# Keys, queries and values of three recurrent scans, turned by VectorE and DMA instead of TensorE

## The chip, the cores and the metric

The kernel runs on one core of a Trainium2 chip. The metric is the device time of one execution in microseconds; lower is better. TensorE (PE) multiplies matrices and writes into PSUM, eight banks of 128x512 floats. VectorE (DVE), ScalarE (ACT) and GpSimd (POOL) work on elements; SyncE (SP) issues every DMA of this kernel, in program order.

## The reference

One layer of a decoder with three kinds of recurrent heads, for a prompt of 1024 tokens with 16 learned tokens in front, and for 8 sequences of 8 tokens. Cut to what matters:

```python
h = _rmsnorm(x, norm_w)
proj = h @ w_in                              # (tokens, 8984): q, k, v, gates and z of 16 heads
conv = silu(causal_conv4(concat[bq, bk, bv]))
qb, kb, vb = _l2norm(q) * 128 ** -0.5, _l2norm(k), v          # DeltaNet, 6 heads
logf, kc, qc, vc = ...                                        # HGRN, 4 heads
ha = mlstm_scan(q, k, v, i_pre, f_pre) * sigmoid(o)           # mLSTM, 6 heads
hb = gated_delta_scan(qb, kb, vb, g, beta)
hc = hgrn_scan(qc, kc, vc, logf)
hcat = head_rms_norm(concat[ha, hb, hc]) * out_norm_w * silu(z)
y = rmsnorm(x + hcat @ w_out)                                 # and the states after the last token
```

Every scan needs its keys in two layouts: the feature on the partitions (to multiply keys with queries over the feature) and the token on the partitions (to sum keys times values over tokens, into the state).

## The kernel before

The prompt is cut into two halves of 512 tokens; the first half also carries a small group of 80 columns, the 64 sample tokens and the 16 learned ones. In each half the weight columns pass in tiles of 128 features. A tile's projection has the features on the partitions and the tokens along the free dimension (tile `acc`; 288 and 304 or 288 and 288 columns in the first half, 512 in the second). To keep float32 precision, each weight piece of 512x128 (`wraw`, four buffers) is split into a rounded part (`whi`, by ScalarE) and the rest (`wlo`, by VectorE), as the activations are (`hA` in the first half, `hB` in the second), and three products are added: 12 products a piece and column range. After the tiles come the output products `oacc`.

When the tiles of a head are done, its scan starts: `mlstm_scan`, `gdn_scan` (DeltaNet) or `hgrn_scan`. A scan works on groups: the main group of four chunks of 128 tokens, and in the first half also the small group. The heads' order is written out by hand (C0, B0, A0, B1, A1, C1, ...; A is mLSTM, B DeltaNet, C HGRN).

Each scan is a Python generator. The emitter keeps a clock of estimated engine times (`ck`), and a scheduler of streams (`Weave`) runs a scan's next step once its due time has passed on TensorE's clock, so that small matmuls of a scan stand between the weight products. `ck.last = ck.t["T"] + 5.0` ahead of a `yield` puts a step off by 5 us of that clock. When a third head would start, the oldest scan is drained: its steps are emitted at once. The framework below then orders instructions by their place in this stream and by its own estimate of when they are ready. All calls to an engine go through one helper, line 138, so the profile shows that line for them; DMAs show their own lines.

Token-major copies are made in two ways. The main groups' mLSTM keys (`pk`), DeltaNet keys, queries and values (`pck`, `pcq`, `pvb`) and HGRN keys after their decay (`pkh`) are transposed on TensorE into PSUM, four 128x128 blocks a group, and read from there. mLSTM's values and output gates and HGRN's values are turned without TensorE already: `turned_evac` lets VectorE transpose 32x32 blocks while it empties `acc`, `turn_out` stores the tile to DRAM in four DMAs of 64 KB whose addresses put the blocks in their places, and `turn_in` loads it with one DMA of 256 KB. `finish`, which normalises a head's output, turns it back in the same way (`yd`). In DeltaNet's chain over the chunks, `pr` is key times state, `pw` the solved product, `pu` the state's update and `po` the output; each needs the one before it. `kwall` holds mLSTM's keys weighted by their gates, `kn` DeltaNet's normed keys.

Of the kernel before, what the change touches and what calls it, by code (L numbers as in the profile page):

```python
# [6 lines left out]
F32 = mybir.dt.float32  # L7
# [4 lines left out]
ALU = mybir.AluOpType  # L12
# [179 lines left out]
def hybrid_step(ctx, tc, i, o):  # L192
# [12 lines left out]
    dp = ctx.enter_context(tc.tile_pool(name="dp", bufs=1, space=bass.MemoryType.DRAM))  # L205

    def row(tag, name, dtype=F32):
        return rp.tile([P, UW], dtype, tag=tag, name=name, bufs=1 if tag in ("u", "k") else 2)

    def sq(tag, name, bufs=2, width=P, dtype=F32):  # L210
        return sp.tile([P, width], dtype, tag=tag, name=name, bufs=bufs)
# [586 lines left out]
                S.activation(t[:, off:off + cnt], a, func, scale=scale)  # L798
        return t

    def turn_out(t, name):

        d = dp.tile([NC * NQ, SQ, NQ, SQ], F32, name=name)
        for q in range(NQ):
            DMA(d[:, :, q].rearrange("x j i -> j x i"), t[SQ * q:SQ * (q + 1), 0:HALF].rearrange("p (x i) -> p x i", i=SQ))
        return d
# [4 lines left out]
    def turned_evac(half, acc, tag, name, small):  # L811
        t = row(tag, name)
        for a, off, cnt in spans(half, acc):
            n = min(cnt, HALF - off)
            V.transpose(t[:, off:off + n], a[:, 0:n])
            if n < cnt:
                small(t[:, HALF:off + cnt], a[:, n:cnt])
        return t, turn_out(t, scratch_name(name))
# [12 lines left out]
    def finish(half, head, outs, ssq, scale, zs):  # L831
        r = sp.tile([P, 16], F32, tag="hr", name="hr")
        for g in half.groups:
            V.tensor_scalar(r[0:g.n, g.idx], ssq[0:g.n, g.idx], scale / P, EPS, op0=ALU.mult, op1=ALU.add)
            G.tensor_tensor(r[0:g.n, 8 + g.at:8 + g.at + g.nt], r[0:g.n, g.idx], halfneg[0:g.n, 0:g.nt], op=ALU.pow)
        yield
        hrs = []
        for g, hx in zip(half.groups, outs):
            hr = gt("6", g)
            rb = r[0:g.n, 8 + g.at:8 + g.at + g.nt].unsqueeze(2).to_broadcast([g.n, g.nt, P])  # L840
            V.tensor_tensor(hr[0:g.n], hx[0:g.n], rb, op=ALU.mult)
            hrs.append(hr)
# [3 lines left out]
        d = turn_out(y, scratch_name("yd"))  # L846
# [118 lines left out]
    def mlstm_scan(half, h, kT, qT, vT, tho, zs, nm, em, st):  # L965
# [10 lines left out]
        Cn = state_A[h]  # L976
        Es, kws, v1s, ogs, hxs = [], [], [], [], []
        kwall = sp.tile([P, 5, P], F32, tag="sB", name="kwall", bufs=1)
        for g in half.groups:
            n = g.n  # L980
            pst = bank("pst")
            for c in range(g.nt):
                T.matmul(g.psum(pst, n)[:, c], g.col(kT, c), g.col(qT, c), start=True, stop=True)
            E = gt("0", g)
            for c in range(g.nt):
                S.activation(E[0:n, c, 0:n], g.col(nm, c)[0:n], AF.Exp, bias=cols[0:n, g.at + c, K_A, h:h + 1])
            ck.sync()
            V.tensor_tensor(E[0:n, :, 0:n], E[0:n, :, 0:n], g.psum(pst, n), op=ALU.mult)
            Es.append(E)
        yield  # L990
        for g in half.groups:
            n = g.n
            pk = bank("pk")
            for c in range(g.nt):
                T.transpose(g.psum(pk)[:, c], g.col(kT, c), ident)
            kw = kwall[:, g.idx]
            V.tensor_tensor(kw[0:n], g.psum(pk), gate_col(half, g, K_W, h), op=ALU.mult)
            kws.append(kw)
            v1 = gt("2", g, P + 1)
            G.memset(v1[0:n, :, P:P + 1], 1.0)  # L1000
            if g.small:
                pv = bank("pv")
                T.transpose(g.psum(pv)[:, 0], g.col(vT[0], 0), ident)
                S.copy(v1[0:n, :, 0:P], g.psum(pv))
            else:
                turn_in(v1[:, :, 0:P], vT[1])
                og = gt("3", g)
                turn_in(og, tho[1])
            v1s.append(v1)
        ck.last += 2.5  # L1010
        yield
# [95 lines left out]
        G.tensor_copy(U[:, 0:3], hist[:, ei])  # L1107
        return U

    def conv_post(half, U, ei, Cv):  # L1110
        base = NB * (NS + 3)
        W = half.width
        co = sq("io", "co")
# [27 lines left out]
        yield  # L1141
        yield
        silu2(Cv[:, 0:W], U[:, 0:W], Cv[:, 0:W])

    def gdn_scan(half, h, ck_, cq, cv, zs, Gb, eG, bb, st):
        W = half.width
# [4 lines left out]
        qd = row("k", "qd")[:, 0:W]  # L1151
        nrm = sp.tile([P, 40], F32, tag="nrm", name="nrm", bufs=1)
        V.memset(nrm, 1.0)
        pks = []
        for g in gs:
            pk, pq = bank("pck"), bank("pcq")
            for c in range(g.nt):
                T.transpose(g.psum(pk)[:, c], g.col(ck_, c), ident)
            for c in range(g.nt):
                T.transpose(g.psum(pq)[:, c], g.col(cq, c), ident)  # L1160
            for off, src in ((0, pk), (5, pq)):
                for c in range(g.nt):
                    scr = sq("scr", "scrq", bufs=1)
                    S.activation(scr[0:g.n], g.psum(src)[:, c], AF.Square, accum_out=nrm[0:g.n, off + g.at + c:off + g.at + c + 1])
# [6 lines left out]
        yield  # L1171
        kns, Es = [], []
        for g, pk in zip(gs, pks):
            kn = gt("4", g)
            V.tensor_tensor(kn[0:g.n], g.psum(pk), nrm[0:g.n, 20 + g.at:20 + g.at + g.nt].unsqueeze(2).to_broadcast([g.n, g.nt, P]), op=ALU.mult)
            kns.append(kn)
        for g in gs:
            E = gt("0", g)
# [73 lines left out]
        def side():  # L1252
            for g, E in zip(gs, Es):
                n = g.n
                pq = bank("pqk")
                for c in range(g.nt):
                    T.matmul(g.psum(pq, n)[:, c], g.col(knT, c), g.col(cq, c), start=True, stop=True)
                Aq = gt("2", g)
                V.tensor_tensor(Aq[0:n, :, 0:n], E[0:n, :, 0:n], g.psum(pq, n), op=ALU.mult)
                Aqs.append(Aq)  # L1260
            yield
            if half.first:
                pr = bank("pkq")
                sample_read_pair(st, kq, pr)
                rds.append(sq("rd", "rd", bufs=1))
                S.copy(rds[0], pr[:, 0:P])
            for g, kn in zip(gs, kns):
                n = g.n
                pv = bank("pvb")
                for c in range(g.nt):  # L1270
                    T.transpose(g.psum(pv)[:, c], g.col(cv, c), ident)
                vb = gt("3", g)
                V.tensor_tensor(vb[0:n], g.psum(pv), gate_col(half, g, K_HB, h), op=ALU.mult)
# [135 lines left out]
    def hgrn_scan(half, h, kT, lf, qT, vT, zs, st):  # L1409
# [97 lines left out]
        for g in gs:  # L1507
# [6 lines left out]
                turn_in(v, vT[1])  # L1514
            vs.append(v)
        yield
        for g in gs:
            pt = bank("pkh")
            for c in range(g.nt):
                T.transpose(g.psum(pt)[:, c], g.col(kd, c), ident)  # L1520
            kk = gt("3", g)
            S.copy(kk[0:g.n], g.psum(pt))
            kks.append(kk)
        yield
        Sm = state_C[h]
        Ss = gt("4", main)
# [66 lines left out]
    def done_tile(half, name, what, acc):  # L1593
# [23 lines left out]
        elif kind == "B":  # L1617
# [5 lines left out]
            c["posts"].append(weave.add("post", conv_post(half, U, ei, t[what]), lag="V"))  # L1623
        else:
            if what == "f":
                cf = evac(half, acc, "f", "cf")[:, 0:half.width]
# [200 lines left out]
```

## Time and profile before

| | |
|---|---|
| median of 3 runs | 2525.58 us (2525.36 to 2528.02) |
| profiled execution | 2525.14 us, its span 2523.4 us |
| mean granted TensorE clock | 0.992 |
| PE / DVE / ACT / POOL busy | 97% / 57% / 40% / 22% |
| DMA queue of SP | 680,828 packets, 348 MB, 53.9% of 16 engines' span |

The rows below come from this one profiled execution. In a timeline row stand the start, the length, the engine and line, the operation with output and inputs, its shape and count, and in brackets how long the engine idled before it and what released it. In a row of waits stand the sum, the number and the longest in microseconds. A group's row has the busy time after the bar, then the mean length of one in ns.

### The profile page before, as it was taken

The page shows a single profiled execution, that of the slowest core. Times are in us where ns is not written, and L with a number is a line of the kernel's source. Part 1 is how long each engine was busy: PE and PEld are TensorE (multiplying, and loading weights), DVE is VectorE, ACT ScalarE, POOL GpSimd, SP SyncE. Part 2 cuts the span into 40 slices and gives each one's busy share as a digit, 9 for nine tenths or more (in the row PEclk, how much of TensorE's full clock was granted, in tenths as well). Part 3 has the DMA queues.
Part 4 walks back from the last instruction along what each step waited for, and adds up shares of the span by engine and source line. Part 5 has one row for each costly group of instructions (what it writes and reads, how often), then busy time and mean ns, then how long its engine had stood idle before and what let it go on. Part 6 is the DMA issues. An engine that isn't in the chain of part 4 may idle for free.

```text
span 2523.4 us, 43205 instructions
## 1 busy us (share of the span) xinstructions
PE 2456.8 (97%) x15702; PEld 2199.6 (87%) x15702; DVE 1427.0 (57%) x2977; ACT 1012.3 (40%) x2476; POOL 555.0 (22%) x722
## 2 busy tenths in 40 slices
PE   6999999999999999999899999999999999999998
PEld 5899999999999999999687888888888888888886
DVE  7775656765746655556854556554554645323435
ACT  5643434343435333343643434333543334322324
POOL 5331211420314212213320103110320102211201
PEclk9999999999999999999999999999999999999999
DMA  5666655656545454448455445454554548636735
GB/s 129 157 143 147 154 135 122 166 135 133 144 97 143 97 128 115 118 105 225 115 134 122 119 121 130 120 132 100 131 128 111 130 118 264 175 83 195 259 96 184
DMA packets 681041, 350.77 MB, mean 139 GB/s; under 512 B 260004, under 2 KB 622076, under 8 KB 680828
## 3 DMA queue, kind: packets, MB, share of 16 engines
q1 hardware_dynamic: 680828, 348.01, 53.9%
q8 instruction: 123, 2.02, 0.3%
q14 instruction: 90, 0.74, 0.1%
HBM read 285.71 MB, written 62.19 MB: 138 GB/s over the span
## 4 chain that ended last, share of the span: by engine, by line
PE 74%; DMA 6%; issue 6%; DVE 5%; ACT 4%; POOL 3%; SPq 1%; POOLq 0%; DVEq 0%; ACTq 0%
PE acc L138 55%; PE oacc L138 8%; PE pa L138 1%; DVE wlo L138 1%; DMA wraw<-in_w_in_dram 1%; PE po L138 1%; POOL X L138 1%; PE pyy L138 1%; PE pz L138 1%; POOL res L138 1%; ACT whi L138 1%; PE pu L138 1%; ACT L138 1%; PE poh L138 1%; PE nd L138 1%
## 5 line engine op out<-in xcount | busy, mean ns | idle before, releaser
L138 DVE TENSOR_TENSOR wlo<-wraw,whi 128x512 fp32r<-128x512 f32 x720 | 528.4, 738 | 584.9 <-ACT whi L138 566.0
L138 PE MATMUL acc<-hA,whi 128*128 128x288 f32 (+1 forms) x4544 | 823.0, 303 | 11.5 <-ACT whi L138 7.0
L138 ACT CAST whi<-wraw 128x512 fp32r<-128x512 f32 x720 | 441.3, 618 | 879.8 <-PE acc L138 570.2
L138 PE MATMUL acc<-hB,whi 128*128 128x512 f32 x2272 | 723.8, 400 | 4.4 <-ACT whi L138 3.2
L138 PEld LDWEIGHTS acc<-hA,whi 128*128 128x128 f32 x4544 | 678.3, 191 | 17.5 <-ACT whi L138 8.4
L138 PE MATMUL acc<-hA,wlo 128*128 128x288 f32 x2240 | 488.9, 298 | 2.1 <-DVE wlo L138 2.0
L138 PEld LDWEIGHTS acc<-hB,whi 128*128 128x128 f32 x2272 | 411.2, 189 | 84.0 <-ACT whi L138 4.0
L138 PE MATMUL acc<-hB,wlo 128*128 128x512 f32 x1120 | 440.5, 393 | 5.1 <-DVE wlo L138 4.9
L138 PEld LDWEIGHTS acc<-hA,wlo 128*128 128x128 f32 x2240 | 367.1, 190 | 2.9 <-DVE wlo L138 2.9
L138 PE MATMUL oacc<-whi,y 128*128 128x512 f32 x1088 | 344.8, 391 | 1.7 <-ACT whi L138 1.6
L138 PEld LDWEIGHTS acc<-hB,wlo 128*128 128x128 f32 x1120 | 210.6, 188 | 55.9 <-DVE wlo L138 10.4
L138 PEld LDWEIGHTS oacc<-whi,y 128*128 128x128 f32 x1088 | 205.0, 188 | 45.6 <-ACT whi L138 3.4
L138 PE MATMUL oacc<-wlo,y 128*128 128x512 f32 x576 | 225.5, 392 | 2.1 <-DVE wlo L138 2.1
L138 PEld LDWEIGHTS oacc<-wlo,y 128*128 128x128 f32 x576 | 108.6, 189 | 26.1 <-DVE wlo L138 3.9
L138 POOL TENSOR_TENSOR res<-res,fnw 128x512 f32<-128x512 f32 (+1 forms) x34 | 54.3, 1624 | 255.3 <-ACT oscr L138 255.3
L138 POOL TENSOR_TENSOR qd<-qT,emb 128x512 f32<-128x512 f32 x12 | 16.8, 1403 | 355.9 <-PE po L138 355.9
L138 POOL TENSOR_TENSOR y<-y,zs 128x592 fp32r<-128x592 f32 (+1 forms) x32 | 45.5, 1420 | 92.4 <-ACT zs L138 62.8
L138 DVE TENSOR_TENSOR Yt<-Yc,Bb 128x60 f32<-128x60 f32 (+8 forms) x180 | 36.7, 204 | 39.4 <-DMA Bb<-db 34.4
L138 POOL TENSOR_TENSOR hr<-hr,halfneg 128x4 f32<-128x4 f32 (+1 forms) x48 | 47.4, 987 | 46.2 <-DVE hr L138 44.7
L138 POOL TENSOR_TENSOR X<-Ex,hk 128x256 f32<-128x256 f32 (+1 forms) x40 | 38.1, 953 | 87.8 <-PE pa L138 67.9
L138 POOL TENSOR_TENSOR nrm<-nrm,halfneg 128x10 f32<-128x10 f32 x12 | 23.5, 1955 | 122.6 <-DVE nrm L138 122.6
L138 DVE TENSOR_TENSOR Sx<-Sx,lf 128x256 f32<-128x256 f32 (+2 forms) x60 | 36.5, 613 | 20.2 <-ACT Ex L138 19.1
(410 smaller groups left out, 2805.8 us busy)
## 6 DMA issues: line engine op xcount, KB each, us to landing
wraw<-in_w_in_dram SPq DMA_DIRECT2D x564, 256.0 KB
wraw<-in_w_out_dram SPq DMA_DIRECT2D x144, 256.0 KB
y<-y SPq DMA_DIRECT2D x16, 576.0 KB
px<-in_x_prompt_dram SPq DMA_DIRECT2D x32, 256.0 KB
yd<-y SPq DMA_DIRECT2D x128, 64.0 KB
out_dram<-sst SPq DMA_DIRECT2D x16, 512.0 KB
s<-yd SPq DMA_DIRECT2D x32, 256.0 KB
y<-zs SPq DMA_DIRECT2D x32, 256.0 KB
```

The lines of the kernel that those rows point to most:

```text
L138: return f(out, *a, **k)
```

## The change

For the main groups the five TensorE transposes go, and the tiles are turned by VectorE and DMA. `turn_tile` now makes the DRAM tile, and `turn_out` stores into one that is given.

DeltaNet: at the end of `conv_post` VectorE transposes the finished tile into its old input buffer `U` (tag `u`, which gets a second buffer), and `turn_out` stores it to `cd`; at the scan's start three `turn_in` load keys, queries and values, and a new step of 5 us is put in. mLSTM: the scan transposes its keys into `kt`, stores them to `kd`, loads values and gates (earlier than before) and `kwall`, and the next step is due no sooner than 7 us later. HGRN: the same for the decayed keys, with 6 us.

```diff
-        return rp.tile([P, UW], dtype, tag=tag, name=name, bufs=1 if tag in ("u", "k") else 2)
+        return rp.tile([P, UW], dtype, tag=tag, name=name, bufs=1 if tag == "k" else 2)
...
+    def turn_tile(name):
+        return dp.tile([NC * NQ, SQ, NQ, SQ], F32, name=scratch_name(name))
+
+    def turn_out(t, d):
...
# mlstm_scan
+        kt = sp.tile([P, HALF], F32, tag="s7", name="kt", bufs=1)
+        V.transpose(kt, kT[:, 0:HALF])
+        dk = turn_tile("kd")
+        turn_out(kt, dk)
+        v1m, og = gt("2", half.main, P + 1), gt("3", half.main)
+        turn_in(v1m[:, :, 0:P], vT[1])
+        turn_in(og, tho[1])
+        turn_in(kwall[:, half.main.idx], dk)
+        ready = ck.t["T"] + 7.0
...
+        ck.last = max(ck.last, ready)
         yield
...
-            pk = bank("pk")
-            for c in range(g.nt):
-                T.transpose(g.psum(pk)[:, c], g.col(kT, c), ident)
...
# conv_post
         silu2(Cv[:, 0:W], U[:, 0:W], Cv[:, 0:W])
+        V.transpose(U[:, 0:HALF], Cv[:, half.base:half.base + HALF])
+        turn_out(U, turned)
...
# gdn_scan
-            pk, pq = bank("pck"), bank("pcq")
-            for c in range(g.nt):
-                T.transpose(g.psum(pk)[:, c], g.col(ck_, c), ident)
-            for c in range(g.nt):
-                T.transpose(g.psum(pq)[:, c], g.col(cq, c), ident)
...
+                pk, pq, vm = gt("4", g), gt("9", g), gt("3", g)
+                turn_in(pk, dk)
+                turn_in(pq, dq)
+                turn_in(vm, dv)
+                ck.last = ck.t["T"] + 5.0
+                yield
...
-                pv = bank("pvb")
-                for c in range(g.nt):
-                    T.transpose(g.psum(pv)[:, c], g.col(cv, c), ident)
...
# hgrn_scan
+        kt = sp.tile([P, HALF], F32, tag="s7", name="kt", bufs=1)
+        V.transpose(kt, kd[:, 0:HALF])
+        dk = turn_tile("kd")
+        turn_out(kt, dk)
...
+                turn_in(kk, dk)
             kks.append(kk)
+        ck.last = ck.t["T"] + 6.0
         yield
```

SP's queue at the scan of the last mLSTM head (A5) in the second half, before: stores of the gates `tho`, weight loads, the loads of gates and values (`s` tiles).

```order
L805 DMA tho_23205<-tho 32x16x32 x4
L239 DMA wraw<-in_w_in_dram 128x4x128 x3
L809 DMA s_23429<-tho_23205 128x4x128
L239 DMA wraw<-in_w_in_dram 128x4x128
L1772 DMA fnw<-in_final_norm_w_dram 128x512
L1385 DMA out_dram<-state_B_751 128x128
L809 DMA s_23426<-vT_23057 128x4x128
L239 DMA wraw<-in_w_in_dram 128x4x128
```

The same place now:

```order
L807 DMA kd_23548<-kt 32x16x32
L239 DMA wraw<-in_w_in_dram 128x4x128
L807 DMA kd_23548<-kt 32x16x32 x2
L239 DMA wraw<-in_w_in_dram 128x4x128
L807 DMA kd_23548<-kt 32x16x32
L1800 DMA fnw<-in_final_norm_w_dram 128x512
L239 DMA wraw<-in_w_in_dram 128x4x128
L811 DMA kwall<-kd_23548 128x4x128
L811 DMA s_23554<-tho_23287 128x4x128
L1800 DMA fnw<-in_final_norm_w_dram 128x512
L811 DMA s_23553<-vT_23181 128x4x128
```

Four stores of `kd` stand among the weight loads, and the load of `kwall`, which needs all four to have landed, stands ahead of the loads of gates and values.

PE in the first half, in DeltaNet's chain over the chunks of head B3 (`state_B_749`), from the third chunk's `pw` to the fourth chunk's `pr`, before:

```order
L138 MATMUL pw<-s_9056,s_9124 128x128
L138 MATMUL acc<-hA_82,whi 128x288
L138 MATMUL acc<-hA_82,whi 128x304
L138 MATMUL acc<-hA_83,whi 128x288
L138 MATMUL acc<-hA_83,whi 128x304
L138 MATMUL acc<-hA_82,wlo 128x288
L138 MATMUL acc<-hA_82,wlo 128x304
L138 MATMUL pu_9761<-Wt,s_8878 128x128
L138 MATMUL po_9763<-state_B_749,qd 128x128
L138 MATMUL po_9763<-Wt,s_9021 128x128
L138 MATMUL acc<-hA_82,whi 128x288
L138 MATMUL acc<-hA_82,whi 128x304
```

The same chain now, from the second chunk's `pu` to the fourth's:

```order
L138 MATMUL po_9890<-state_B_749,qd 128x128
L138 MATMUL po_9890<-Wt,s_9206 128x128
L138 MATMUL pr<-state_B_749,knT 128x128
L138 MATMUL pw<-s_8883,s_9309 128x128
L138 MATMUL pu_9904<-Wt,s_8881 128x128
L138 MATMUL po_9906<-state_B_749,qd 128x128
L138 MATMUL po_9906<-Wt,s_9206 128x128
L138 MATMUL pr<-state_B_749,knT 128x128
L138 MATMUL pw<-s_8883,s_9309 128x128
L138 MATMUL pu_9920<-Wt,s_8881 128x128
L138 MATMUL po_9922<-state_B_749,qd 128x128
L138 MATMUL po_9922<-Wt,s_9206 128x128
```

The weight products that stood between the steps of two chunks are gone from between them.

More of the change, by code (lines that the diff above doesn't have):

```diff
@@ L992, in mlstm_scan @@
             n = g.n
-            pk = bank("pk")
-            for c in range(g.nt):
-                T.transpose(g.psum(pk)[:, c], g.col(kT, c), ident)
-            kw = kwall[:, g.idx]
-            V.tensor_tensor(kw[0:n], g.psum(pk), gate_col(half, g, K_W, h), op=ALU.mult)
+            kw = pk = kwall[:, g.idx]
+            if g.small:
+                pk = bank("pk")[:, 0:P].unsqueeze(1)
+                T.transpose(pk[0:n, 0], g.col(kT, 0), ident)
+            V.tensor_tensor(kw[0:n], pk[0:n], gate_col(half, g, K_W, h), op=ALU.mult)
             kws.append(kw)
-            v1 = gt("2", g, P + 1)
+            v1 = gt("2", g, P + 1) if g.small else v1m
             G.memset(v1[0:n, :, P:P + 1], 1.0)
@@ L1004, in mlstm_scan @@
                 S.copy(v1[0:n, :, 0:P], g.psum(pv))
[L1005 to L1008, printed above, removed]
             v1s.append(v1)
@@ L1108, in conv_evac, with conv_post @@
         return U
-    def conv_post(half, U, ei, Cv):
+    def conv_post(half, U, ei, Cv, turned):
         base = NB * (NS + 3)
@@ L1153, in gdn_scan @@
         V.memset(nrm, 1.0)
+        (ck_, dk), (cq, dq), (cv, dv) = ck_, cq, cv
         pks = []
         for g in gs:
-            pk, pq = bank("pck"), bank("pcq")
-            for c in range(g.nt):
-                T.transpose(g.psum(pk)[:, c], g.col(ck_, c), ident)
-            for c in range(g.nt):
-                T.transpose(g.psum(pq)[:, c], g.col(cq, c), ident)
+            if g.small:
+                pk, pq = (bank(n)[0:g.n, 0:P].unsqueeze(1) for n in ("pck", "pcq"))
+                T.transpose(pk[:, 0], g.col(ck_, 0), ident)
+                T.transpose(pq[:, 0], g.col(cq, 0), ident)
+            else:
+                pk, pq, vm = gt("4", g), gt("9", g), gt("3", g)
[4 more added lines that the diff above has]
+                yield
             for off, src in ((0, pk), (5, pq)):
@@ L1173, in gdn_scan @@
         for g, pk in zip(gs, pks):
-            kn = gt("4", g)
-            V.tensor_tensor(kn[0:g.n], g.psum(pk), nrm[0:g.n, 20 + g.at:20 + g.at + g.nt].unsqueeze(2).to_broadcast([g.n, g.nt, P]), op=ALU.mult)
+            kn = gt("4", g) if g.small else pk
+            V.tensor_tensor(kn[0:g.n], pk, nrm[0:g.n, 20 + g.at:20 + g.at + g.nt].unsqueeze(2).to_broadcast([g.n, g.nt, P]), op=ALU.mult)
             kns.append(kn)
@@ L1268, in side @@
                 n = g.n
-                pv = bank("pvb")
-                for c in range(g.nt):
-                    T.transpose(g.psum(pv)[:, c], g.col(cv, c), ident)
-                vb = gt("3", g)
-                V.tensor_tensor(vb[0:n], g.psum(pv), gate_col(half, g, K_HB, h), op=ALU.mult)
+                if g.small:
+                    pv = bank("pvb")[0:n, 0:P].unsqueeze(1)
+                    T.transpose(pv[:, 0], g.col(cv, 0), ident)
+                    vb = gt("3", g)
+                else:
+                    pv = vb = vm
+                V.tensor_tensor(vb[0:n], pv, gate_col(half, g, K_HB, h), op=ALU.mult)
                 vbs.append(vb)
@@ L1516, in hgrn_scan @@
         yield
+        kt = sp.tile([P, HALF], F32, tag="s7", name="kt", bufs=1)
+        V.transpose(kt, kd[:, 0:HALF])
+        dk = turn_tile("kd")
+        turn_out(kt, dk)
         for g in gs:
-            pt = bank("pkh")
-            for c in range(g.nt):
-                T.transpose(g.psum(pt)[:, c], g.col(kd, c), ident)
             kk = gt("3", g)
-            S.copy(kk[0:g.n], g.psum(pt))
+            if g.small:
+                pt = bank("pkh")
+                T.transpose(g.psum(pt)[:, 0], g.col(kd, 0), ident)
+                S.copy(kk[0:g.n], g.psum(pt))
+            else:
+                turn_in(kk, dk)
             kks.append(kk)
+        ck.last = ck.t["T"] + 6.0
         yield
@@ L1622, in done_tile @@
             t[what] = row({"k": "c", "q": "d", "v": "f"}[what], "C" + what)
-            c["posts"].append(weave.add("post", conv_post(half, U, ei, t[what]), lag="V"))
+            d = turn_tile("cd")
+            c["posts"].append(weave.add("post", conv_post(half, U, ei, t[what], d), lag="V"))
+            t[what] = t[what], d
         else:
```

8 lines of the change are left out of this document (3 added, 5 removed).

## The prediction

> **What bounds the kernel now.** I read the head of the page first: how full each engine is, and the clock that TensorE was granted in each fortieth of the span.
>
> ```profile
> span 2523.4 us, 43205 instructions
> PE 2456.8 (97%) x15702; PEld 2199.6 (87%) x15702; DVE 1427.0 (57%) x2977; ACT 1012.3 (40%) x2476; POOL 555.0 (22%) x722
> PE   6999999999999999999899999999999999999998
> PEclk9999999999999999999999999999999999999999
> PE 74%; DMA 6%; issue 6%; DVE 5%; ACT 4%; POOL 3%; SPq 1%; POOLq 0%; DVEq 0%; ACTq 0%
> ```
>
> TensorE (PE) is busy in 97% of the span and carries 74% of the chain that ended last. A busy PE is no proof by itself, so two stretches were asked for by windows (columns: start and end, length, busy time and instructions of PE, PEld, DVE, ACT, POOL, then the clock granted), and then the longest waits.
>
> ```profile
> 440.00:700.00 260.00, 258.13 (x2055) 254.45 (x2054) 168.38 (x360) 107.97 (x305) 74.61 (x100) 1.00 0.60 143
> 1260.00:2090.00 830.00, 827.16 (x4511) 687.18 (x4510) 453.05 (x934) 321.64 (x769) 143.68 (x152) 1.00 0.50 124
> ...
> ACT whi L138 <- PE acc L138: 570.2, 313, 4.3
> ACT whi L138 <- DMA wraw<-in_w_in_dram: 26.4, 15, 7.4
> ```
>
> In the first half of the tokens PE idles 2 us of 260, in the second 3 us of 830. ScalarE's weight copies (whi) wait 570 us for PE to free a buffer and only 26 us for the weights to arrive. So PE, fed in program order, is the limit, and a PE instruction removed shortens the run by the time from its start to the next one's start, as long as nothing else makes PE wait.
>
> **What leaves PE.** The change takes away the four 128x128 transposes of each main group, five kinds of them:
>
> ```profile
> L138 PE MATMUL pcq<-ident,Cq 128*128 128x128 f32 x48 | 7.2, 273 | 0.0
> L138 PE MATMUL pk<-ident,kT 128*128 128x128 f32 x48 | 7.2, 272 | 0.0
> L138 PE MATMUL pvb<-ident,Cv 128*128 128x128 f32 x48 | 7.2, 272 | 0.0
> L138 PE MATMUL pck<-ident,Ck 128*128 128x128 f32 x48 | 7.2, 272 | 0.0
> L138 PE MATMUL pkh<-ident,hkd 128*128 128x128 f32 x32 | 4.8, 272 | 0.0
> ```
>
> That is 224 transposes, 56 groups of four, 28 in each half. Their busy time, 33.6 us, counts the pipeline's end of each group, so it is an upper end; the price is read from starts. From the timeline of PE, second half and then first half:
>
> ```profile
> 2077.38 0.60 PE L138 MATMUL pk<-ident,kT 128*128 128x128 f32 x4
> 2077.73 0.71 PE L138 MATMUL acc<-hB,whi 128*128 128x512 f32 x2
> 2078.28 0.40 PE L138 MATMUL acc<-hB,wlo 128*128 128x512 f32 x1
> 2078.51 0.62 PE L138 MATMUL acc<-hB,whi 128*128 128x512 f32 x2
> 2078.97 0.39 PE L138 MATMUL acc<-hB,wlo 128*128 128x512 f32 x1
> ...
> 190.36 0.27 PE L138 MATMUL pcq<-ident,Cq 128*80 128x128 f32 x1
> 190.47 0.60 PE L138 MATMUL pck<-ident,Ck 128*128 128x128 f32 x4
> 190.90 0.60 PE L138 MATMUL pcq<-ident,Cq 128*128 128x128 f32 x4
> 191.26 0.79 PE L138 MATMUL acc<-hA,whi 128*128 128x288 f32 x4
> ```
>
> In the second half the four start 0.35 us ahead of the next weight product (2077.38 to 2077.73), and that pair then takes 0.55 us to the next start where an undisturbed pair takes 0.46 (2078.51 to 2078.97): 0.35 + 0.09 = 0.44 us a group. In the first half eight transposes take 0.79 us (190.47 to 191.26), 0.40 a group; the stretched pair behind them stays, since the small group's transposes stay on PE. 28 x 0.44 + 28 x 0.40 = **23.5 us** off PE.
>
> **What is added, and what hides it.** Every group of four becomes one VectorE transpose in 32x32 blocks, four stores to DRAM and one load back. The kernel already does this for other tiles, so rows exist (the tile's VectorE form, the SP queue's timeline, SP's waits, the page's queue line):
>
> ```profile
> L138 DVE STREAM_TRANSPOSE y<-s x32: 697/706/712, 182.9 to 2178.8; 128x512 f32<-128x512 f32 x32
> ...
> 2075.19 1.95 SPq L805 DMA_DIRECT2D yd<-y  x4
> 2081.78 0.37 SPq L809 DMA_DIRECT2D s<-yd  x1
> ...
> SPq L809 <- DMA yd<-y: 9.0, 16, 1.7
> q1 hardware_dynamic: 680828, 348.01, 53.9%
> ```
>
> VectorE: 56 x 0.706 = 39.5 us more on an engine that is busy 57% of the time. It waits for PE and ScalarE far longer than that, so I cost this at nothing; if that cover went, wlo would be late next. ScalarE loses eight pkh copies, which frees nothing that is waited for. SP: 56 x (1.95 + 0.37) = 130 us more of issuing, spread over some 2100 us. The new waits stand here: a load waits until its stores have landed, and in the mLSTM and HGRN scans it is issued soon after them, with weight loads (wraw) queued behind. The nearest row is the load of yd: 16 waits, 9.0 us in all, 1.7 at most. A weight piece lasts 12 products of 0.23 us, 2.8 us, in the second half, and wraw is four buffers deep, so some 11 us may pass: nothing, against an upper end of 12 x 1.7 + 8 x 1.7 = 34 us if no buffer covered it. DMA engines: 56 x (4 x 512 + 512) = 143,360 packets more; at this queue's mean cost that adds 11 points to 53.9%, by bytes (29 MB on 348) 4.5 points. Either leaves room. U's second buffer (tag u) and eight matmul banks held for a shorter time can only help; I cost them at nothing.
>
> VectorE: DVE Perf Modes in the Trainium skill, section "The three transpose paths", speaks against the change: it calls a plain strided DMA 19 times slower than the crossbar transpose's 1309 ns, an estimated 25 us a block. The trace does not agree for this pattern: four stores and their landing fit in under 5 us.
>
> **What the new order costs.** The scans now wait longer for their data by the emitter's clock (5 us in DeltaNet, 6 to 7 in the others), and the scheduler lays PE's order out anew. Nearly everywhere scan products still stand between weight products. For two heads of the first half, B2 and B3, they don't: there pr, pw, pu and the next pr follow each other with no weight product between. I count 15 such bare hand-overs (2 at pyy-px-pz, 4 and 3 in B2's chain, 6 in B3's), where the kernel before has weight products at each. At each, PE ends a product, VectorE or ScalarE works on it, and PE waits. Priced by a covered chain step and by two bare hand-overs of before:
>
> ```profile
> 258.94 0.38 PE L138 MATMUL pr<-state_B,knT 128*128 128x128 f32 x2
> 259.36 0.35 DVE L138 SCALAR_TENSOR_TENSOR s<-pr,cols,s 128x128 f32<-128x128 f32 x1 [0.51 <-PE pr L138]
> 261.95 0.27 ACT L138 COPY Wt<-pw 128x128 f32<-128x128 f32 x1 [0.63 <-PE pw L138]
> ...
> 201.20 0.37 PE L138 MATMUL pkk<-knT 128*80 128x80 f32 x2 [0.93 <-ACT knT L138]
> 202.30 1.01 PE L138 MATMUL pkk<-knT 128*128 128x128 f32 x3 [0.73 <-ACT knT L138]
> ```
>
> pr starts at 258.94 and ends at 259.32; s is done at 259.71: at least 0.4 us idle. The pkk rows show 0.93 and 0.73. I take 0.45, since the chain's own operations (0.35 and 0.27 us) are the small ones: 15 x 0.45 = **6.8 us**; the ends are 3 (if PE is late there anyway) and 14.
>
> Such idle time costs twice, by the granted clock (windows, PEclk is the third column from the end):
>
> ```profile
> 196.00:203.00 7.00, 4.95 (x33) 4.23 (x32) 2.63 (x9) 2.64 (x8) 4.83 (x5) 0.90 0.66 169
> 203.00:210.00 7.00, 7.00 (x39) 7.00 (x39) 3.56 (x8) 1.21 (x4) 0.83 (x2) 0.61 0.25 74
> 288.00:293.00 5.00, 2.15 (x26) 1.67 (x22) 4.81 (x11) 1.32 (x7) 3.78 (x5) 1.00 0.17 51
> 293.00:298.00 5.00, 5.00 (x25) 4.82 (x26) 5.00 (x23) 3.20 (x13) 1.89 (x3) 0.66 0.63 158
> ...
> 292.96 0.46 PE L138 MATMUL nd<-s,qd 128*128 128x129 f32 x2 [1.77 <-DVE s L138]
> ```
>
> After 2.0 us idle in 196 to 203 the clock was 0.61 over the next 7 us, a loss of 2.7; after 2.9 us in 288 to 293 it was 0.66 over 5 us, a loss of 1.7. Both B2's chain and B3's hold as much idle time, so 2 x 2.2 = **4.4 us** (0 to 8).
>
> TensorE: Matmul & The Clock Gate in the Trainium skill ("Why this matters for your kernels") asks only for no idle gaps over about 3 us. By it these gaps would leave the clock alone and the sum would be 4.4 us lower. The trace does not agree: no single gap here passes 1.8 us, and the clock falls.
>
> **Sum.** The profiled execution took 2525.14 us, 0.4 below the median of the runs: 2525.1 - 23.5 + 6.8 + 4.4 = 2512.8; on the median's scale **2513 us**. A change under 0.2%, 5 us, is about what a measurement of this kernel can't tell from none.
>
> **Rivals.**
> A, the whole saving stays: PE comes to the bare places late or the weights are late there in any case. 2525.1 - 23.5 = 2502. For it: both stretches above hide scans wholly. Against: the order is fixed, and a hand-over can't be shorter than VectorE's 0.35 us.
>
> B, slower: the turned tiles arrive later than the scans were laid out for, so that PE stops in every scan at the first product that needs one (pkT, pum, puh).
>
> ```profile
> DVE Yt L138 <- DMA Bb<-db: 34.4, 12, 5.6
> PE nd L138 <- DVE s L138: 4.8, 4, 1.8
> ```
>
> For it: db's round trip through DRAM, given 7 us too, still kept VectorE waiting 2.9 us on average. Against: no PE wait names it, and the yd turns cost PE nothing. It decides from 23.5 / 32 = 0.73 us in each of the 32 scans; at 1.2 us, as in the nd row, 32 x 1.2 = 38 us, and 2525 - 23 + 38 = 2540.
>
> C, no change: bare hand-overs at the upper end (14 us) and a third fall of the clock (3 x 2.7 = 8 us) use up 22 of the 23.5: 2524.
>
> The Trainium skill's price (VectorE: DVE Perf Modes, "The three transpose paths"), an estimated 25 us a block, would make B hold, each scan some 18 us late; the yd row is against it.
>
> **Numbers.** Forecast 0.52, A 0.22, C 0.14, B 0.12. Faster holds the forecast and A; C is the same: 0.74, 0.14, 0.12. The range reaches from A less the 2.9 us gap of 288 to 293, which the new order may lose, to C with 3 us of waits on SP: 2499 to 2527.
>
> **What would show it.** Right: no 128x128 pck, pcq, pk, pvb, pkh left in the groups; PE's busy time down by 25 to 34 us; PE idle inside B2's and B3's chains with a clock under 1 behind it; the second half shorter by about 12 us with no new PE wait; STREAM_TRANSPOSE up by 40 us. Wrong: PE waits at pkT, pum or puh in many scans (B), whi waiting for wraw much over 26 us (SP holds the weights back), or several falls of the clock outside B2 and B3.

## The result, and the profile after

The change made the kernel slower: 2605.07 us (median of 4, 2602.65 to 2612.67) against 2526.24 (4 runs, 2525.36 to 2528.02), a ratio of 1.0316 (1.0294 to 1.0339). The profiled execution took 2603.79 us, 78.7 us of span more. The head of its page:

```profile
span 2602.1 us, 43171 instructions
PE 2460.6 (95%) x15478; PEld 2189.5 (84%) x15478; DVE 1478.1 (57%) x3033; ACT 1004.4 (39%) x2466; POOL 560.1 (22%) x722
PE   6999999998889999999799999999999999999998
PEclk8999999999999999999899999999999999999999
q1 hardware_dynamic: 828668, 377.39, 57.9%
```

PE runs 224 instructions fewer and is yet busy 4 us longer, since more of its work ran at half clock. The two stretches that stood for "PE is fed" before, and the place with the worst slices (619 to 853 us; the same weight products as 614 to 805 before), by windows, columns as above:

```profile
440.00:700.00 260.00, 241.44 (x1862) 234.28 (x1860) 165.72 (x353) 94.50 (x266) 65.37 (x89) 0.97 0.60 140
619.00:853.00 234.00, 202.79 (x1485) 193.86 (x1484) 127.10 (x279) 79.89 (x220) 35.37 (x58) 0.93 0.56 130
1300.00:2120.00 820.00, 797.21 (x4198) 654.98 (x4199) 473.12 (x943) 313.34 (x745) 151.49 (x156) 1.00 0.57 137
```

PE idles 19 us of 260, 31 of 234, 23 of 820. Before, the middle stretch took 191 us, so 43 of the 79 us lie there; another 18 lie in the first third of the second half's products. What PE waits for (sum, number, longest):

```profile
PE acc L138 <- ACT whi L138: 24.8, 12, 8.4
PE px L138 <- DVE s L138: 16.6, 11, 2.9
PE pkT L138 <- DVE t L138: 11.8, 4, 7.4
PE pt L138 <- DVE x L138: 11.8, 7, 6.4
PE acc L138 <- DVE wlo L138: 9.6, 12, 1.6
PE puh L138 <- issue: 7.3, 1, 7.3
PE pkT L138 <- DVE s L138: 7.0, 7, 2.0
PE oacc L138 <- ACT whi L138: 6.4, 3, 5.6
...
ACT whi L138 <- DMA wraw<-in_w_in_dram: 37.1, 21, 5.2
```

Before, pkT, px and puh waited 2.5 us together, the two largest rows being:

```profile
PE px L138 <- DVE s L138: 1.1, 1, 1.1
PE pkT L138 <- DVE t L138: 0.4, 1, 0.4
```

pkT and puh are products that rival B names (pt waited as long before). Of these rows only puh's, 7.3 us, is a wait for a turned tile that came late. Then the two longest waits, each with what stands ahead of it (whi, then pkT):

```profile
661.49 0.70 DVE L138 STREAM_TRANSPOSE xT<-px 128x512 f32<-128x512 f32 x1
662.23 0.62 ACT L138 CAST px<-xT 128x512 fp32r<-128x512 f32 x1 [3.88 <-DVE xT L138]
663.42 0.86 PE L138 MATMUL acc<-hA,whi 128*128 128x288 f32 x2 [8.37 <-ACT whi L138]
...
738.91 0.69 DVE L138 TENSOR_TENSOR s<-s,cols 128x512 f32<-128x512 f32 x1 [3.27 <-DMA s<-cd]
740.80 0.70 ACT L138 COPY qT<-acc 128x288 f32<-128x288 f32 x2 [6.90 <-PE acc L138]
748.33 0.40 PE L138 MATMUL pkT<-ident,t 80*128 80x80 f32 x1 [7.43 <-DVE t L138]
```

At 663.42 the weights had landed: whi stands in ScalarE's order behind px, which itself waited 3.9 us for VectorE. Of the 24.8 us that PE waited for whi, 5.1 us, in two waits, lead to a landing of weights. At 748.33 the turned tiles had been loaded by 738.9; between lie ScalarE's squares for the norm of the keys, held up behind qT, then POOL and VectorE. So these long waits come out of chains between the engines, and not out of a landing that came late for the product itself; in before_delays, below, PE waits at pkT with nothing new turned.

One accounting serves all that follows. From a page: idle = span less PE's busy time; lost to the clock = span x (1 - mean granted clock), the clock being 1.0 or 0.5 in every record; full-speed work = busy less lost.

| kernel | span | busy | idle | clock | lost | full-speed work |
|---|---|---|---|---|---|---|
| before | 2523.4 | 2456.8 | 66.6 | 0.992 | 20.2 | 2436.6 |
| changed | 2602.1 | 2460.6 | 141.5 | 0.981 | 49.4 | 2411.2 |
| before_delays | 2558.2 | 2467.0 | 91.2 | 0.990 | 25.6 | 2441.4 |
| before_plus_turns | 2566.7 | 2461.5 | 105.2 | 0.988 | 30.8 | 2430.7 |
| before_no_transposes | 2517.3 | 2434.3 | 83.0 | 0.990 | 25.2 | 2409.1 |
| ..._same_order | 2506.4 | 2428.8 | 77.6 | 0.993 | 17.5 | 2411.3 |

So 25.4 us of work did leave PE, and 74.9 us of idle time and 29.2 us of lost clock came in. The first, third and fourth rows have the same work on PE and give 2436.6, 2441.4 and 2430.7, so a figure of this table is good to some 5 us.

### The profile page after: what moved, and what is told of

The parts are those of the page before. It is cut to its first block, busy times and chain, and to the rows that moved or that the text cites. A ratio compares the mean times of both kernels' runs of the same rounds, so it can differ in the third digit from the quotient of the medians.

```text
span 2602.1 us, 43171 instructions
## 1 busy us (share of the span) xinstructions
PE 2460.6 (95%) x15478; PEld 2189.5 (84%) x15478; DVE 1478.1 (57%) x3033; ACT 1004.4 (39%) x2466; POOL 560.1 (22%) x722
## 5 line engine op out<-in xcount | busy, mean ns | idle before, releaser
L138 ACT ACTIVATE scrq<-s 128x128 f32<-128x128 f32 x224 | 69.1, 309 | 11.7 <-DVE s L138 6.9
L138 DVE TENSOR_TENSOR Yt<-Yc,Bb 128x60 f32<-128x60 f32 (+8 forms) x180 | 36.0, 200 | 34.3 <-DMA Bb<-db 29.2
L138 POOL TENSOR_TENSOR vx<-v,quadmask 128x512 fp32r<-128x512 f32 x16 | 18.2, 1139 | 161.8 <-ACT v L138 126.6
```

The lines of the kernel that those rows point to most:

```text
L138: return f(out, *a, **k)
```

## The experiments

Differences are between medians measured together; ratios have their 95% intervals.

**Late or put off?** after_nodelay takes out the three put-offs, before_delays puts them alone into the kernel before.

```diff
# after_nodelay
-                ck.last = ck.t["T"] + 5.0
-                yield
-        ready = ck.t["T"] + 7.0
+        ready = ck.t["T"] + 0.0
-        ck.last = ck.t["T"] + 6.0
# before_delays, at the same three steps
+        ck.last = ck.t["T"] + 5.0
+        yield
...
+        ready = ck.t["T"] + 7.0
+        ck.last = max(ck.last, ready)
...
+        ck.last = ck.t["T"] + 6.0
```

> The changed kernel with its turns, but without the three put-offs of 5, 7 and 6 us on the emitter's clock (and without DeltaNet's extra step). Changed kernel 2605, kernel before 2526; with the 23.5 us that leave PE, something costs 102 us. Theory 'planned delay' (the put-offs alone move scan steps behind the point where a third head drains them, so that they stand bare in PE's order): the put-offs gone, about 2505 to 2535, and the waits at pkT and px fall back to the 1 to 2 us of before. Rival 'late data' (turned tiles reach the scan later than its place in PE's order): every first use is now placed 5 to 7 us earlier, so more waits, 2605 to 2680, with PE waiting at pkT in all 12 DeltaNet scans and at pum, puh. Rival 'added work' (VectorE, SP and DMA loads hold up the weights): unchanged, 2590 to 2615.

Measured: 2616.89, +93.8 us (1.0367, 1.0349 to 1.0384). Not only put-offs, then; PE waits longer without them:

```profile
PE pum L138 <- DMA yd<-y: 25.1, 1, 25.1
PE pkT L138 <- DVE t L138: 20.6, 5, 6.1
PE pkT L138 <- DVE s L138: 19.1, 9, 5.0
```

The first row is one stall behind a background store, of the kind shown under before_plus_turns below. At pkT PE waits 39.7 us instead of 18.8. ScalarE now waits three times, 6.4 us, for the loads of the keys, which the changed kernel's put-offs had covered; the rest at pkT is again the chain of the norm.

> The kernel before, TensorE transposes and all, with nothing added but the three put-offs of 5, 7 and 6 us on the emitter's clock at the same steps. 'Planned delay': slower than before by most of what the change lost, 2590 to 2630 (the 224 transposes are still there). 'Late data': the data are there at once, so 2526 to 2540. 'Added work': nothing is added, 2521 to 2531.

Measured: 2561.45, +38.3 us (1.0149, 1.0132 to 1.0167). That lies between the ranges given for "planned delay" (2590 to 2630) and "late data" (2526 to 2540): the put-offs cost half the loss with none of the new turns in the program:

```profile
PE pkT L138 <- DVE t L138: 7.0, 3, 2.5
PE pkT L138 <- DVE s L138: 6.6, 3, 2.3
PE pum L138 <- issue: 6.2, 6, 1.4
PE pum L138 <- DVE kwall L138: 5.9, 4, 1.7
```

A likely reason, read from the code and not counted in a trace: a scan that starts 5 to 7 us later has more steps left when a third head starts, and these are then emitted one after the other, with no weight product between.

**The parts.** Each kernel turns only one head type's tiles and takes the other functions from the kernel before.

```diff
# b_only: mlstm_scan and hgrn_scan of before; a_only and c_only: gdn_scan, conv_post and done_tile
# of before, and hgrn_scan or mlstm_scan; in a_only and c_only tag u as before
-        return rp.tile([P, UW], dtype, tag=tag, name=name, bufs=1 if tag == "k" else 2)
+        return rp.tile([P, UW], dtype, tag=tag, name=name, bufs=1 if tag in ("u", "k") else 2)
```

> Only DeltaNet's keys, queries and values are turned (36 of the 56 groups, its put-off of 5 us kept); mLSTM and HGRN as before. If each part costs by itself: PE gains 36 x 0.42 = 15 us. 'Planned delay': 12 scans put off by 5 us, a bit under half of all put-off time, 2550 to 2580. 'Late data': the DeltaNet waits of the changed kernel (pkT 19 us, px 17 us, and the clock halved behind them, some 10 us) stay, 2550 to 2575. 'Added work': 36/56 of it, 2560 to 2580. It is run for the size of the part.

> Only mLSTM's keys are turned (12 of the 56 groups, its put-off of 7 us kept). PE gains 12 x 0.42 = 5 us. 'Planned delay': 12 scans put off, 2535 to 2560. 'Late data': PE waits at pum for kwall in the scans, up to 12 x 2.8 us (the longest wait at pum in the changed kernel), 2525 to 2555. 'Added work': 12/56 of the loss, 2535 to 2550. It is run for the size of the part.

> Only HGRN's decayed keys are turned (8 of the 56 groups, its put-off of 6 us kept). With DeltaNet alone 45 us slower and mLSTM alone 4, some 30 us of the 79 are left: if the parts add up, HGRN alone costs 2545 to 2560. If the loss comes from the queue on SP, which every part fills and where the parts meet, HGRN alone costs little, 2520 to 2535, and the rest of the loss belongs to the parts together. PE gains 3.4 us.

Measured: DeltaNet 2568.61, +45.5 (1.0176, 1.0156 to 1.0196); mLSTM 2527.36, +4.2 (1.0012, 1.0003 to 1.0022); HGRN 2551.59, +30.0 (1.0126, 1.0110 to 1.0143). They add up to 79.7. HGRN's eight groups cost as much as two thirds of DeltaNet's 36, so the loss doesn't follow the amount of work. HGRN's data are made in the scan itself, right ahead of the step that needs them, and this explains the 8.9 us that PE waits at puh with HGRN alone turned. It doesn't explain the 8.4 us that PE then waits at pkT, in DeltaNet's scans, where nothing new is turned; how the rest of the 30 us divides is open, since each part also has an order of its own. For the same reason the sum of 79.7 proves little. At the start of the second half of the changed kernel (DVE, SP, PE):

```profile
1246.56 0.69 DVE L138 STREAM_TRANSPOSE kt<-hkd 128x512 f32<-128x512 f32 x1
1250.81 2.68 SPq L239 DMA_DIRECT2D wraw<-in_w_in_dram  x4
1253.59 0.76 SPq L811 DMA_DIRECT2D s<-hvT  x1
1256.82 3.10 SPq L239 DMA_DIRECT2D wraw<-in_w_in_dram  x4
1259.97 2.84 SPq L807 DMA_DIRECT2D kd<-kt  x4
1262.90 0.69 SPq L239 DMA_DIRECT2D wraw<-in_w_in_dram  x1
1265.43 0.38 SPq L811 DMA_DIRECT2D s<-kd  x1
1268.31 2.05 PE L138 MATMUL puh<-s,s 128*128 128x128 f32 x8 [7.32 <-issue]
```

The tile is turned at 1247.25; its stores go out 12.7 us later, behind eight weight loads, and puh starts 21.1 us after the turning where 6 were planned. In mLSTM's 12 scans the time from the turned tile to its use by VectorE was 16.3 to 67 us where 7 were planned. PE hardly felt that: it waited 2.1 us for kwall, and with mLSTM alone turned the time rose by 4.2 us.

**The added work without a reader, and the removed work without a substitute.** before_plus_turns keeps the TensorE transposes and adds VectorE's transposes, the stores and the loads (into a tile `idle`, three of a tile's four chunks). before_no_transposes lets the readers take the untransposed tile, and in the second form the emitter still counts the time of the missing transposes.

```diff
# before_plus_turns, one of three places
+        kt = sp.tile([P, HALF], F32, tag="s7", name="kt", bufs=1)
+        V.transpose(kt, kT[:, 0:HALF])
+        idle_in(turn_out(kt, turn_tile("kd")))
# before_no_transposes, one of five places (main groups)
-            for c in range(g.nt):
-                T.transpose(g.psum(pk)[:, c], g.col(kT, c), ident)
-            V.tensor_tensor(kw[0:n], g.psum(pk), gate_col(half, g, K_W, h), op=ALU.mult)
+            V.tensor_tensor(kw[0:n], g.psum(pk) if g.small else g.cols(kT), gate_col(half, g, K_W, h), op=ALU.mult)
# ..._same_order, in its place
+                    ck.run("T", 0.06 + P * 0.0004)
```

> The kernel before, TensorE transposes and all, with the work of the turns on top: VectorE's 56 transposes, their 224 stores and 56 loads on SP (loads of three of the four chunks, 192 KB, for want of space), into a tile that nobody reads, without put-offs, and with U's second buffer. It asks what the added work costs when no one waits for its data. 'Late data' and 'planned delay': little, 2523 to 2540 (VectorE and SP have room). 'Added work' (VectorE, SP's queue and the DMA engines hold up the weights): most of the loss, 2560 to 2625.

Measured: 2569.93, +45.5 us (1.0180, 1.0164 to 1.0195). Nobody waits for `idle`, yet it costs as much as DeltaNet's part: neither of the first two theories holds alone. One stall makes up more than half of it (SP, DVE, ACT, SP again, PE; A2's scan):

```profile
639.19 0.44 SPq L927 DMA_DIRECT2D sst<-in_state_mlstm_C_dram  x1
652.60 0.67 DVE L138 STREAM_TRANSPOSE xT<-px 128x512 f32<-128x512 f32 x1
653.30 0.62 ACT L138 CAST px<-xT 128x512 fp32r<-128x512 f32 x1 [2.25 <-DVE xT L138]
653.94 1.95 SPq L643 DMA_DIRECT2D hbhi<-px  x4
658.65 2.14 SPq L807 DMA_DIRECT2D kd<-kt  x4
662.92 0.38 SPq L811 DMA_DIRECT2D idle<-kd  x1
665.38 0.50 SPq L811 DMA_DIRECT2D s<-vT  x1
668.44 0.77 PE L138 MATMUL pum<-s,kwall 128*128 128x129 f32 x2 [25.69 <-DMA s<-vT]
```

The background step that prepares the second half's activations (`prep_B`) stores hbhi and hblo, 128 stores in all. SP stands 14.3 us at one of them until VectorE and ScalarE have made it. Behind it stand the turn's stores and load, and behind these the load of values that PE's next product needs. The twelfth of the first half's weight products in which this lies takes 128.6 us, against 94.6 before: 34.0 of the 43.3 us by which the profiled span is longer. Elsewhere the added work costs some 9 us.

The changed kernel has the same trouble at the same place: SP stands up to 14.3 us at such a store, and this twelfth takes 116.3 us; in after_nodelay 10.2 us and 133.0. Before, SP stood there at most 3.4 us, and in before_delays, with the new order's put-offs but no new turns, the twelfth takes 91.7.

> The kernel before, with the main groups' 224 TensorE transposes left out and nothing in their place: whoever read the transposed tile in PSUM reads the untransposed one in SBUF. It leaves part of the computation out and gives the price of the transposes alone. The prediction's price: 23.5 us, 2500 (2496 to 2505). If the transposes covered hand-overs of the scans that now stand bare, less is saved: 2505 to 2520.

Measured: 2519.83, -4.6 us (0.9984, 0.9975 to 0.9994). By the table 27.5 us of work left PE, and 21.4 came back as idle time and lost clock.

> The kernel before without the main groups' 224 transposes and with nothing in their place (readers take the untransposed tile, which leaves part of the computation out), as before_no_transposes, but the emitter's clock still counts the transposes' estimated time, so that every scan step comes in the same place of the program as in the kernel before. before_no_transposes took 27 us of full-speed work off PE and gained 4 us, since idle time rose by 16 us and the loss by a halved clock by 5. If the new order took the gain back, the old one gives 2500 to 2508 here. If PE's queue has no slack at these places in any order (the time goes into waits for VectorE and ScalarE in the scans), 2514 to 2522.

Measured: 2512.36, -12.3 us (0.9949, 0.9937 to 0.9961), between the two expectations. The new order takes some 8 us; in the old one, too, half the saving goes into waits.

**Another queue.** The new turns' DMAs issued by POOL, by ACT; then, with the turns on SP, the stores of hbhi and hblo issued by ACT, with a control.

```diff
# after_act_queue (after_pool_queue: nc.gpsimd)
+    DMA2 = nc.scalar.dma_start
-        turn_out(kt, dk)
+        turn_out(kt, dk, DMA2)
# after_prep_act, before_prep_act
-                    DMA(d[g, :, :, at_:at_ + SQ].bitcast(F32).rearrange("x j i -> j x i"),
+                    nc.scalar.dma_start(d[g, :, :, at_:at_ + SQ].bitcast(F32).rearrange("x j i -> j x i"),
```

> The changed kernel with the DMAs of its new turns (the stores of cd and kd, and their loads) issued by POOL instead of SP; the older turns and the weights stay on SP. In the changed kernel a tile of mLSTM's keys is multiplied by its gates 16.3 to 67 us after VectorE turned it (7 were planned), since its four stores and its load stand in SP's queue among weight loads that wait for a free wraw buffer. Theory 'late by SP's queue': off that queue the round trip falls to 5 to 9 us, and the time to that of the put-offs alone less the transposes, 2561 - 23.5 = 2538 (2525 to 2560). Rival 'late by the DMAs themselves' (runs of 128 B take long to land, whoever issues them): the round trip stays above 12 us and the time at 2590 to 2620. Rival 'POOL pays' (POOL's own work for the scans stands behind the DMAs' waits): the round trip falls, but the time stays at 2570 to 2620 with new waits on POOL.

Measured: 2849.76, +325.3 us (1.1280, 1.1263 to 1.1297), beyond all the ranges given. POOL issues slowly:

```profile
1499.46 0.65 POOL L808 DMA_DIRECT2D kd<-kt  x1 [1.87 <-issue]
1501.99 0.66 POOL L808 DMA_DIRECT2D kd<-kt  x1 [1.88 <-issue]
1504.52 0.65 POOL L808 DMA_DIRECT2D cd<-U  x1 [1.87 <-issue]
```

One DMA each 2.53 us, where SP takes 0.5: the rival "POOL pays", and more than it expected.

> The same with ACT as the issuer. 'Late by SP's queue': the round trip falls where ACT is free, but ACT's copies of the weights (whi) wait behind stores that wait for VectorE and loads that wait for landing: 2535 to 2590. 'Late by the DMAs themselves': 2590 to 2620. If ACT's waits decide, PE waits at acc for whi well over the 24.8 us of the changed kernel, and 2600 to 2660.

Measured: 2570.61, +46.2 us (1.0174, 1.0155 to 1.0193), some 33 us better than the changed kernel, each against the kernel before, with no byte moved differently. The twelfth with the stall takes 92.7 us. The mLSTM round trip fell to 12.0 to 14.4 us.

> The changed kernel with one thing moved: the 128 stores of hbhi and hblo (the second half's activations, prepared in the background of the first half, line 643) are issued by ACT instead of SP. The turns stay on SP. In the changed kernel 43 of the 79 us lie between two thirds and three fifths of the first half's products (619 to 853 us), where these stores still run; in the kernel before with the turns' work added, SP stood 14.3 us at such a store, which waited for ACT and VectorE, with the load that PE's next product needed behind it (PE idle 25.7 us). Theory 'SP's one queue' (DMAs that wait for an engine hold back the loads behind them): that stretch returns to 190 to 200 us and the time to 2560 to 2580. Rival 'the turns are late by themselves' (their own four stores and load behind each other and the weights): 2590 to 2610.

> Control: the kernel before with the same stores of hbhi and hblo issued by ACT. If they hold nothing back there, 2520 to 2528; if they do already, faster, 2505 to 2520; if issuing costs ACT time that PE waits for, 2528 to 2540.

Measured: 2569.18, +47.6 (1.0187, 1.0170 to 1.0204), and the control 2531.62, +10.0 (1.0042, 1.0027 to 1.0057). The stretch that held 43 us of the loss is nearly as before (first before, then after_prep_act):

```profile
614.00:805.00 191.00, 188.61 (x1511) 185.23 (x1510) 113.67 (x271) 81.70 (x228) 43.81 (x61) 1.00 0.53 129
631.50:827.80 196.30, 191.86 (x1489) 187.42 (x1488) 112.49 (x258) 78.27 (x214) 35.00 (x57) 0.97 0.50 125
```

The twelfth with the stall takes 91.9 us. In the profiled executions the control is 8 us late by the first sixth of the first half's products, ahead of any of these stores, and ends 5 us late: the order was laid out anew there too. Either way of parting the turns from these stores returns 31 to 33 us, and the stretch that they mend is the one in which SP stood. Each also shifts the whole order, so it isn't shown that every microsecond of these was a wait on SP itself.

**Can it gain at all, and what is an order worth?** early_turns and early_mlstm turn mLSTM's keys as soon as they leave acc:

```diff
+                    kt = row("u", "kt")
+                    V.transpose(kt[:, 0:HALF], t[what][:, 0:HALF])
+                    t[what] = t[what], turn_out(kt, turn_tile("kd"))
```

> A version built from what the runs showed: mLSTM's keys turned and stored as soon as they leave acc (some 50 us ahead of the scan) and loaded at the scan's start without a put-off; DeltaNet's as in the changed kernel with 2 us of put-off instead of 5; HGRN's keys on TensorE as before; the turns' and the hbhi and hblo stores' DMAs issued by ACT. PE gains 48 groups, 20 us. If lateness and put-offs are the whole loss: 2510 to 2525. If ACT's waits for the stores cost PE: 2530 to 2560. If what is left is the new order (hand-overs that the transposes and the older order covered): 2525 to 2545.

Measured: 2557.98, +36.4 (1.0153, 1.0132 to 1.0174); in spite of 2 us of put-off, px (21.6 us) and pkT (16.1) still wait in DeltaNet.

> mLSTM's keys alone turned (12 groups), as soon as they leave acc, some 50 us ahead of the scan, loaded at the scan's start, no put-off, and the emitter's clock counts the transposes as before, so that the order is that of the kernel before; all on SP; tag u with two buffers. PE loses 12 x 0.42 = 5 us of work. If lateness, put-offs and order were the whole loss: 2517 to 2522. If the 48 stores and 12 loads more on SP cost by themselves: 2525 to 2540.

Measured: 2531.92, +7.3 (1.0032, 1.0020 to 1.0044): even early, in the old order, the turns cost more than the 5 us they take off PE.

> The kernel before with one number changed: each scan step is due 0.5 us after the one ahead of it on the emitter's clock, not 0.4. No work is added, removed or made late. If any other order costs (this one is tuned to its numbers), 2540 to 2570, by more idle time where a third head starts; if only put-offs of several microseconds matter, 2521 to 2532.

> The kernel before with each scan step due 0.3 us after the one ahead of it on the emitter's clock, not 0.4. If the time follows the put-off (0.5 cost 16 us), 2505 to 2520, faster than both kernels. [...]

```diff
-LATENCY = 0.4
+LATENCY = 0.5
```

(0.3 in the second.) Measured: 2541.01, +16.4 (1.0067, 1.0054 to 1.0080), and 2528.55, +4.9 (1.0024, 1.0015 to 1.0033). No version that does the whole computation beat the kernel before.

## Why the prediction was wrong, point by point

- **What leaves PE, 23.5 us: right as work** (25.4 by the table), **wrong as time.** "A PE instruction removed shortens the run by the time to the next one's start" failed: removed alone, the transposes gave 4.6 us, and 12.3 with the order kept. They seem to have been cover themselves for the scans' hand-overs: without them PE's idle time grew by 16 and 11 us.
- **The added work "costed at nothing": the step that failed most, 45.5 us** when done alone. VectorE's 39.5 us were sized right (the five new forms sum to 39.4 us; first and last):

```profile
L138 DVE STREAM_TRANSPOSE U<-Cv 128x512 f32<-128x512 f32 x12 | 8.5, 709 | 0.5
L138 DVE STREAM_TRANSPOSE kt<-hkd 128x512 f32<-128x512 f32 x8 | 5.6, 700 | 1.1 <-POOL hkd L138 1.1
```

  The error is in SP's sentence. The nearest row, 1.7 us at most, was the wait for landing, the last link only; the wait in the queue in front of the stores and of the load was left out. In the very rows shown, yd's first store was issued at 2075.19 and its load at 2081.78: 6.6 us from the start of the stores to the load, so "four stores and their landing fit in under 5 us" holds only without the queue. Between the two stood weight loads, in a row that the prediction passed over:

```profile
2077.24 4.37 SPq L239 DMA_DIRECT2D wraw<-in_w_in_dram  x3
```

  The upper end of 34 us was still too low, because it priced SP's waits one by one, not what else stands behind them, which here was the load that PE's next product needed. Most of the 45.5 us, some 34, came from this one place.
- **"What the new order costs", 11.2 us (6.8 + 4.4): the put-offs alone cost 38.3.** The counted hand-overs were right in size, B3's chain for example (PE):

```profile
640.33 0.49 PE L138 MATMUL pw<-s,s 128*128 128x128 f32 x2 [0.45 <-DVE s L138]
641.18 0.49 PE L138 MATMUL pu<-Wt,s 128*128 128x128 f32 x2 [0.35 <-ACT Wt L138]
```

  but "nearly everywhere scan products still stand between weight products" was read from which products adjoin in PE's order. Whether the data behind a covered product are there in time can't be seen in an order; pkT and px come after long chains of ScalarE and VectorE work, and with the put-offs alone PE already waits 13.6 us at pkT. Why the put-offs cost 38.3 us is not fully shown: a new order of any kind can cost something here, 16.4 us for a change of 0.1 us in one number, and that share wasn't separated.
- **Sum of the three:** 38.3 + 45.5 - 4.6 = 79.2 us, measured 78.8. The closeness is luck: the stall of 25.7 us that makes up most of the 45.5 isn't in the changed kernel in that form (its longest PE wait is 8.4 us), and two fixes of SP's queue alone each return 31 to 33 us. How the loss divides between put-offs and queue inside the changed kernel is open.
- **Rival B** held, at 0.12. Its direction was right, its mechanism only in part: puh waits for turned tiles, 9.0 us in all, but the long waits at pkT and for whi come out of chains of the engines, and kwall's delay costs PE 2.1 us. Its price of 1.2 us in each scan was wrong: the waits are in few scans, up to 8.4 us at a time. That it named the right sign is mostly luck. "The yd turns cost PE nothing" was no evidence against it, since a finished head's output has time and a scan's key does not. A and C assumed that the turns were in time.
- **The clock:** 4.4 us (0 to 8) predicted, 29.2 measured. TensorE: Matmul & The Clock Gate in the Trainium skill ("Why this matters for your kernels") warns of idle gaps over some 3 us; here the trace agrees as far as it goes: behind the gaps of 8.37 and 7.43 us the clock was 0.55 over the next 3.6 us and 0.54 over the next 4.0. A gap of that length isn't needed, though: from 643 to 650 us the clock was 0.53 with no gap over 1.4 us ahead of it, as in the prediction's own rows. The 4.4 us counted the falls in B2's and B3's chains and none elsewhere.
- **The Trainium skill's price** of an estimated 25 us a block (VectorE: DVE Perf Modes, "The three transpose paths") was near the shorter of the mLSTM round trips by its size, but not by its cause: with the turns issued by ACT they fell to 12.0 to 14.4 us.
- **What would show it:** STREAM_TRANSPOSE rose as forecast, the five forms left (only the small groups' remain), and two signs of "wrong" came: waits at pkT and puh (though few, and pkT's for another reason), and falls of the clock outside B2 and B3. whi's wait for wraw rose only to 37.1 us.

## What to carry to other kernels

A DMA's price on one in-order queue is the wait of everything in front of it plus the delay of everything behind it; add up issue, queue, landing and load against the time at which the first reader needs the tile. Work taken off a full engine shortens the run only where what stood behind it was ready; take it out alone, with nothing in its place, before building the substitute. Where an order is laid out by numbers, measure what a harmless change of one number costs (here 0.1 us: 16 us) before crediting any edit with a few microseconds.

## What the runs showed of the hardware

POOL issues a strided 64 KB DMA each 2.53 us, SP in about 0.5 (2.14 us for four kd stores above), and POOL's 29.38 MB went in 11,648 packets, ACT's in 147,840. DMA: Bandwidth & Descriptors in the Trainium skill ("Issuing engines are not separate DMA queues") says that another issuer saves only the time of issuing, usually small. Here 280 DMAs, an estimated 130 us of issuing by the rows of SP in the prediction, went to ACT, and the time fell by some 33 us. Whether that was the issuing itself or the loads that no longer stood behind a waiting store isn't separated, and the order of the instructions changed with it.
